# Products paired on row halves in the first mixer, and a class-ordered copy written by ScalarE in the dilated mixer

## The chip, the cores and the metric

The kernel runs as one program on one core of a Trainium2 chip. Five engines matter: TensorE (PE: matrix products; PEld is its weight loads), VectorE (DVE), ScalarE (ACT), GpSimd (POOL) and SyncE (SP), which issues the DMAs. Each works through its own queue in order and waits on semaphores for the others. The metric is the device time of one execution in microseconds; the median of three runs of the kernel before is 3385.5 us (3381.23 to 3389.09).

## What is computed

Two transformer blocks run one after the other on 512 tokens of width 1024. The first has two layers: a mixer and a convolutional FFN each. Its first layer's mixer joins a chunked gated linear attention and a differential attention; its second layer's mixer is a dilated attention. The second block (FFNs, a grouped-query attention with pooling, a gated MLP mixer) is not touched by the change. What the change touches, cut short:

```python
# gated linear attention, chunks of 64 tokens, 4 heads, dk = 64, dv = 128
att = jnp.where(causal, jnp.einsum('bhnik,bhnjk->bhnij', q_d, k_d), 0.0)
o_intra = jnp.einsum('bhnij,bhnjv->bhniv', att, vc)
o = o_intra + jnp.einsum('bhnik,bhnkv->bhniv', q_d, states)      # state product

# differential attention, 4 heads of two parts c, dh = 64, blocks of 128 queries
s = jnp.einsum('bhcqd,bhckd->bhcqk', qblk, kt)                   # score products
p = jax.nn.softmax(jnp.where(kpos[None, :] <= qpos[:, None], s, -jnp.inf), axis=-1)
w = p[:, :, 0] - lam * p[:, :, 1]

# dilated attention: three patterns (128, 1), (512, 4), (2048, 16); dilation 4 and 16 read
# keys, queries and values by residue class of the token (to_class)
```

## The kernel before

Activations stand with features on the 128 partitions and tokens along the row. Each weight product is done three times at reduced precision: operands are split into a high and a low part (`hh`, `hl`, `whi`, `wlo`, `mh`, `ml`), and high by high, low by high and high by low are summed (`mm3`, tiles `gm` and `gt`). ScalarE writes the high part of a weight tile (`whi`), VectorE the rest (`wlo`), from `raw` buffers that SyncE's DMAs fill; a new `raw` is loaded once the `wlo` that read the old one is done. Small products inside the mixers are plain float32; in the trace each of them is two matmul records, called two passes below.

The order of every engine's instructions is settled when the program is built. Mixers are written as tasks (Python generators), and a planner keeps a clock for each engine with a cost for each operation (class `Clock`). After every group of weight products (`tick`) it lets those tasks take a step whose inputs should be ready by TensorE's planned time, if enough of the eight PSUM banks are free. A task that ends earlier or later in the planned time, or takes its banks in another order, so moves the rows of all engines near it.

In the first mixer (`even_mixer`) `diff_unit` does one block of 128 queries of one head of the differential attention: for each of the two parts j it forms scores of `w` = 128, 256, 384 or 512 keys (tile `ds`, contraction over 64 of the 128 rows: rows 0 to 63 for j = 0, 64 to 127 for j = 1), adds the causal mask by a product with the identity (`mc`), then the softmax: a maximum (`mx`) and its scaled negative (`nb`) on VectorE, the exponential (`dp`) on ScalarE. VectorE then joins the two parts (`drc`, `dr2`, `dp`), TensorE transposes (`dt`), ScalarE evacuates, TensorE multiplies by the values (`po`). There are 4 heads by 4 blocks, 16 units. `gla_out` forms the output of one head of the gated linear attention, in four token tiles: a product over 128 rows (`oa<-att,av`), then one or two state products over 64 rows (`oa<-qd,state`), an evacuation (`oraw`); `o_norm` follows it (`osq`, `ss`, `hv`, `rb`).

In the dilated mixer (`odd_mixer`) the first pattern's keys, queries and values come first. After the queries the class-ordered copy of h (`hp`, tiles `ph` and `pl`, 16 tiles of 128x512) is written, which the second and third pattern read. VectorE then has four key norms (`k_norm`: `hv`, `ksq`, `rb`, `ok`) and four query scales (`q_scale`: `qv`, `cc`, `rs_t`, twelve small operations each) to do before the first softmax of the scores `os` (`nbs`, `pr`).

Of the kernel before, what the change touches and what calls it, by code (L numbers as in the profile page):

```python
# [14 lines left out]
AF = mybir.ActivationFunctionType  # L15
# [4 lines left out]
P = 128  # L20
# [4 lines left out]
NK = D // P  # L25
# [156 lines left out]
class Kern:  # L182
# [706 lines left out]
    def even_mixer(self):  # L889
        nc = self.nc  # L890
        h = self.hx
        H = [(h, S)]
        w = lambda i: ("ev_w_in", i)
        toks = [slice(t * P, (t + 1) * P) for t in range(4)]
        lam = self.cp.tile([P, 1], F32, name="lamv")
        kn, qs = {}, {}
        kh, qh = [], []
        pre = self.firsts([w(8), w(9), w(6)])
        for b in range(2):
            for m, ps in enumerate(pre[b]):  # L900
                kr = self.evac(ps, "bk")
                kh.append(self.spawn(self.k_norm(kr, kn, 2 * b + m, self.v("dk_gain"), self.c("bones"), 64, S)))
        for b in range(2):
            for m, ps in enumerate(pre[2] if b == 0 else [p[0] for p in self.gemm(w(7), NK, H)]):
                qh.append(self.q_scale(ps, qs, 2 * b + m, self.v("dq_gain"), self.c("bones2"), 2, 64))
        self.spawn(self.lam(lam))
        bv = [self.g("bv") for _ in range(4)]
        for b in range(2):
            for t, p in enumerate(self.gemm_tok(w(10 + b), NK, h, toks)):
                nc.scalar.activation(bv[t][:, b * 256:(b + 1) * 256], p, AF.Copy)  # L910
        ob, oa = {}, {}
        dn = []
        for hd in range(4):
            o = self.g("dor")
            us = [self.spawn(self.diff_unit(hd, n, qs, kn, bv, lam, o), (qh[hd], kh[hd])) for n in range(4)]
            dn.append(self.spawn(self.o_norm(o, ob, hd, self.v("diff_gain"), 1.0 - (0.8 - 0.6 * math.exp(0.0))), us))

        ps = self.gemm(("ev_w_ar",), NK, H, widths=(16,))[0][0]
        ar = self.g("ar")
        nc.vector.memset(ar[0:17], 1.0)  # L920
        nc.scalar.activation(ar[0:16], ps[0:16], AF.Copy)
        gs = {}
        la = self.spawn(self.log_decay(ar, gs))
        gs["q"] = [self.evac(p[0], "qd", scale=0.125) for p in self.gemm(w(0), NK, H)]
        gs["k"] = [self.evac(p[0], "kr") for p in self.gemm(w(1), NK, H)]
        gs["av"] = av = [self.g("av") for _ in range(4)]
        for b in range(2):
            for t, p in enumerate(self.gemm_tok(w(2 + b), NK, h, toks)):
                nc.scalar.activation(av[t][:, b * 256:(b + 1) * 256], p, AF.Copy)
        gl = self.spawn(self.gla(gs), [la])  # L930
        sg = []
        for b in range(2):
            for m, ps in enumerate(self.gemm(w(4 + b), NK, H)):
                t = self.g("sg")
                nc.scalar.activation(t, ps[0], AF.Silu)
                sg.append(t)
        self.tables(LNEXP)
        gn = [self.spawn(self.gla_out(gs, hd, sg[hd], oa), [gl]) for hd in range(4)]
        self.finish(dn)
        self.proj_out("ev_w_out", None, [ob[i] for i in range(4)], first=4)  # L940
        self.finish(gn)
        self.final(("ev_w_out",), [oa[i] for i in range(4)], None)
# [91 lines left out]
    def diff_unit(self, hd, n, qs, kn, v, lam, o):  # L1034
        nc = self.nc
        q, cc = qs[hd]
        k = kn[hd]
        w = (n + 1) * P
        pr, sm = [], self.s("dsm", 2)
        for j in range(2):  # L1040
            s = self.ps("ds", w)
            r = slice(j * 64, j * 64 + 64)
            self.mm(s, q[r, n * P:(n + 1) * P], k[r, :w], stop=False)
            self.mm(s[:, n * P:], self.mbf["ident"], self.mbf["mc"], start=False)
            p = self.g("dp")
            nb = self.s("nb", 1)
            self.softmax(s, cc[:, 2 * n + j:2 * n + j + 1], p[:, :w], sm[:, j:j + 1], nb)
            pr.append(p)
        yield
        rc = self.s("drc", 2)  # L1050
        nc.vector.reciprocal(rc, sm)
        r2 = self.s("dr2", 1)
        nc.vector.tensor_mul(r2, rc[:, 1:2], lam)
        nc.vector.tensor_scalar(pr[1][:, :w], pr[1][:, :w], r2, None, op0=OP.mult)
        nc.vector.scalar_tensor_tensor(pr[0][:, :w], pr[0][:, :w], rc[:, 0:1], pr[1][:, :w],
                                       op0=OP.mult, op1=OP.subtract)
        yield
        pt = self.ps("dt")
        for j in range(n + 1):
            nc.tensor.transpose(pt[:, j * P:(j + 1) * P], pr[0][:, j * P:(j + 1) * P], self.ident)  # L1060
        wt = pr[1]
        nc.scalar.activation(wt[:, :w], pt[:, :w], AF.Copy)
        yield
        po = self.ps("po", P)
        for j in range(n + 1):
            self.mm(po, v[j][:, hd * P:(hd + 1) * P], wt[:, j * P:(j + 1) * P], start=(j == 0), stop=(j == n))
        nc.scalar.activation(o[:, n * P:(n + 1) * P], po, AF.Copy)
        yield
# [101 lines left out]
                    st[c, n + 1] = prev = s  # L1170
                yield

    def gla_out(self, gs, hd, sg, oa):
        nc = self.nc
        av, att, st, qd = gs["av"], gs["att"], gs["st"], gs["q"]
        c, r = hd // 2, slice((hd % 2) * 64, (hd % 2) * 64 + 64)
        o = self.g("oraw")
        for t in range(4):
            p = self.ps("oa", P)
            self.mm(p, av[t][:, hd * P:(hd + 1) * P], att[t][:, hd * P:(hd + 1) * P], stop=False)  # L1180
            ns = [n for n in (2 * t, 2 * t + 1) if n]
            for n in ns:
                self.mm(p[:, (n % 2) * 64:(n % 2) * 64 + 64], st[c, n][r, :], qd[c][r, n * 64:n * 64 + 64],
                        start=False, stop=(n == ns[-1]))
            nc.scalar.activation(o[:, t * P:(t + 1) * P], p, AF.Copy)
            yield
        yield from self.o_norm(o, oa, hd, self.v("gla_gain"), gate=sg)


    def odd_mixer(self):  # L1190
        nc, a = self.nc, self.a
        h = self.hx
        w = lambda i: ("od_w_in", i)

        def cls(x):
            return x.rearrange("p (r m) -> p r m", r=4)

        def clsps(x):
            return x.rearrange("p (m r) -> p r m", r=4)
# [4 lines left out]
        prob, kt, qs = {}, {}, {}  # L1204
        su, val = [], {}
        hp = []

        def values(gi, b, hh):
            if b == 0:
                val[gi] = [self.g("ov") for _ in range(4)]  # L1210
            sls = [slice(t * P, (t + 1) * P) for t in range(4)]
            for t, p in enumerate(self.gemm_tok(w(gi * 6 + 4 + b), NK, hh, sls)):
                nc.scalar.activation(val[gi][t][:, b * 256:(b + 1) * 256], p, AF.Copy)

        for gi in range(3):
            kh = []
            if gi == 0:
                pk = self.firsts([w(2), w(3), w(0)])
            H = [(hp if gi else h, S)]
            for b in range(2):  # L1220
                for m, ps in enumerate(pk[b] if gi == 0 else [p[0] for p in self.gemm(w(gi * 6 + 2 + b), NK, H)]):
                    k = self.g("ok")
                    nc.scalar.activation(k, ps, AF.Copy)
                    kh.append(self.spawn(self.k_norm(k, kt, (gi, 2 * b + m), self.v("od_k_gain"), self.ones, 128, S)))
            for b in range(2):
                for m, ps in enumerate(pk[2] if gi == b == 0 else [p[0] for p in self.gemm(w(gi * 6 + b), NK, H)]):
                    hd = 2 * b + m
                    qh = self.q_scale(ps, qs, (gi, hd), self.v("od_q_gain"), self.ones[:, 0:1], 1, 128)
                    prob[gi, hd] = [self.g("pr0"), self.g("pr1")] if gi == 0 else [self.g("pr")]
                    su.append(self.spawn(self.odd_scores(gi, hd, kt, qs, prob[gi, hd], sms, nbs), (kh[hd], qh)))  # L1230
            if gi == 0:

                for xs in h:
                    hp.append((self.h("ph"), self.h("pl")))
                    for x, y in zip(xs, hp[-1]):
                        nc.gpsimd.tensor_copy(cls(y), clsps(x))
                for b in range(2):
                    values(0, b, h)

        values(1, 0, hp)  # L1240
        self.finish(su)
        gs = {}
# [611 lines left out]
```

## Time and profile before

| what | value |
|---|---|
| median of three runs | 3385.5 us |
| the profiled execution, its own time | 3386.47 us |
| its span in the trace | 3384.7 us |
| mean granted TensorE clock | 0.993 of full speed |
| PE busy | 3327.9 us (98%) |
| PEld busy | 2898.5 us (86%) |
| DVE busy | 2113.2 us (62%) |
| ACT busy | 1251.6 us (37%) |
| POOL busy | 28.0 us (1%) |
| differential attention, from the first to the last score product | about 107 to 185 us |
| outputs of the gated linear attention | 244 to 280 us |
| class-ordered copies on POOL | 724.8 to about 747 us |

Busy time is the time in which an engine has an instruction under way; TensorE's matmuls overlap in their pipeline, so for its speed one compares the starts of consecutive rows. The granted clock has two levels in the trace, 1.2 and 2.4 GHz, shown as 0.5 and 1.0. All records carry the line of one helper (L172), so groups are told apart by the tiles' names: `ds<-bk,q` writes `ds` from `bk` and `q`.

### The profile page before, as it was taken

The numbers are of one execution on the slowest core, as the hardware profiler recorded it, in microseconds if no ns is written. First come the engines' busy times: TensorE is split into PE (matmuls) and PEld (weight loads), VectorE is DVE, ScalarE is ACT, GpSimd is POOL, SyncE is SP. The second block draws the span as 40 slices with busy tenths as digits, with TensorE's granted clock in tenths as the row PEclk, the third lists the DMA queues.
The fourth block names the chain that finished last, engine by engine and source line by source line (L and its number), as shares of the span: only waits on it lengthen the run. The fifth ranks groups of instructions, "written<-read, shape, count | busy, mean of one in ns | idle before, by whom it ended". The sixth has DMA issues, their size and how long they took to land.

```text
span 3384.7 us, 48370 instructions
## 1 busy us (share of the span) xinstructions
PE 3327.9 (98%) x19172; PEld 2898.5 (86%) x19172; DVE 2113.2 (62%) x4570; ACT 1251.6 (37%) x2526; POOL 28.0 (1%) x29
## 2 busy tenths in 40 slices
PE   7999999989999999999999989999999999999999
PEld 7688888888898888988888987988898889998888
DVE  5757988775669778764455867855663335463333
ACT  5554434334454334322112356422333223443231
POOL 0000000020000000000000000000000000000000
PEclk9999999999999999999999999999999999999999
DMA  3122444412224444443333311344532233222332
GB/s 112 63 63 80 128 141 131 131 63 74 70 88 125 132 136 131 129 146 111 125 119 119 94 42 44 122 153 144 163 100 85 95 100 100 94 89 93 100 99 70
DMA packets 105845, 355.73 MB, mean 105 GB/s; under 512 B 12673, under 2 KB 18962, under 8 KB 105618
## 3 DMA queue, kind: packets, MB, share of 16 engines
q1 hardware_dynamic: 105618, 352.64, 33.2%
q8 instruction: 150, 2.46, 0.3%
q14 instruction: 77, 0.63, 0.1%
HBM read 350.50 MB, written 2.10 MB: 104 GB/s over the span
## 4 chain that ended last, share of the span: by engine, by line
PE 89%; DVE 6%; ACT 3%; issue 1%; DMA 1%; SPq 0%; DVEq 0%; ACTq 0%
PE gm L172 81%; PE gt L172 4%; ACT ap L172 1%; PE ds L172 1%; DVE wlo L172 1%; PE ss L172 1%; DVE nt L172 1%; PE oa L172 1%; DVE amx L172 0%; DVE rs_t L172 0%; PE os L172 0%; ACT L172 0%; DVE ksq L172 0%; DVE x L172 0%; PE opo L172 0%
## 5 line engine op out<-in xcount | busy, mean ns | idle before, releaser
L172 PE MATMUL gm<-hh,whi 128*128 128x512 f32 (+1 forms) x2872 | 1041.0, 362 | 4.9 <-ACT hh L172 4.1
L172 PE MATMUL gm<-hl,whi 128*128 128x512 f32 (+1 forms) x2872 | 1034.5, 360 | 1.2 <-DVE hl L172 1.2
L172 PE MATMUL gm<-hh,wlo 128*128 128x512 f32 (+1 forms) x2872 | 1031.9, 359 | 3.5 <-DVE wlo L172 3.4
L172 DVE TENSOR_TENSOR wlo<-raw,whi 128x512 fp32r<-128x512 f32 (+1 forms) x1028 | 661.7, 681 | 91.9 <-ACT whi L172 91.5
L172 ACT ACTIVATE whi<-raw 128x512 fp32r<-128x512 f32 (+1 forms) x1028 | 581.4, 617 | 291.6 <-PE gm L172 104.8
L172 PEld LDWEIGHTS gm<-hh,wlo 128*128 128x128 f32 x2872 | 543.9, 189 | 87.1 <-DVE wlo L172 4.2
L172 PEld LDWEIGHTS gm<-hh,whi 128*128 128x128 f32 x2872 | 544.7, 190 | 73.5 <-ACT hh L172 4.4
L172 PEld LDWEIGHTS gm<-hl,whi 128*128 128x128 f32 x2872 | 544.7, 190 | 68.4 <-DVE hl L172 1.8
L172 PE MATMUL gm<-mh,whi 128*128 128x512 f32 (+1 forms) x1696 | 577.5, 341 | 0.0
L172 PE MATMUL gm<-ml,whi 128*128 128x512 f32 (+1 forms) x1696 | 573.5, 338 | 1.2 <-DVE ml L172 1.2
L172 PE MATMUL gm<-mh,wlo 128*128 128x512 f32 (+1 forms) x1696 | 572.1, 337 | 0.0
L172 DVE TENSOR_TENSOR ga<-ga,gm 128x512 f32<-128x512 f32 (+1 forms) x110 | 68.1, 633 | 497.5 <-PE gm L172 328.4
L172 PEld LDWEIGHTS gm<-mh,wlo 128*128 128x128 f32 x1696 | 322.2, 190 | 34.8
L172 PEld LDWEIGHTS gm<-ml,whi 128*128 128x128 f32 x1696 | 322.5, 190 | 29.4 <-DVE ml L172 1.6
L172 PEld LDWEIGHTS gm<-mh,whi 128*128 128x128 f32 x1696 | 322.4, 190 | 29.1 <-issue 0.9
L172 ACT ACTIVATE ga<-gm 128x512 f32<-128x512 f32 (+1 forms) x110 | 58.8, 554 | 715.9 <-PE gm L172 715.9
L172 DVE SCALAR_TENSOR_TENSOR macc<-rawm,sc,macc 128x256 f32<-128x256 f32 x504 | 244.0, 484 | 15.4
L172 DVE SCALAR_TENSOR_TENSOR x<-gm,modt,x 128x256 f32<-128x256 f32 (+1 forms) x184 | 106.0, 608 | 226.3 <-PE gm L172 226.2
L172 PEld LDWEIGHTS gm<-hc,whi 128*128 128x128 f32 x736 | 136.0, 190 | 29.0 <-ACT whi L172 1.6
L172 DVE SCALAR_TENSOR_TENSOR cy<-gm,vec,cy 128x511 f32<-128x511 f32 (+1 forms) x176 | 127.8, 747 | 47.9 <-ACT cy L172 44.7
L172 PE MATMUL gm<-hc,whi 128*128 128x256 f32 x736 | 146.2, 282 | 1.4 <-ACT whi L172 1.4
L172 ACT ACTIVATE nsq<-x 128x256 f32<-128x256 f32 x160 | 60.8, 416 | 179.4 <-DVE x L172 175.9
(300 smaller groups left out, 3530.7 us busy)
## 6 DMA issues: line engine op xcount, KB each, us to landing
raw<-in_ffn_w_dram SPq DMA_DIRECT2D x256, 512.0 KB, 4.3
rawm<-in_w_mod_dram SPq DMA_DIRECT2D x144, 512.0 KB, 4.4
raw<-in_ffn_w_up_dram SPq DMA_DIRECT2D x88, 512.0 KB, 3.7
raw<-in_ffn_w_down_dram SPq DMA_DIRECT2D x40, 512.0 KB, 3.7
raw<-in_od_w_in_dram SPq DMA_DIRECT2D x36, 512.0 KB, 3.8
raw<-in_ev_w_in_dram SPq DMA_DIRECT2D x24, 512.0 KB, 3.9
raw<-in_w_in_c_dram SPq DMA_DIRECT2D x16, 512.0 KB, 4.1
raw<-in_w_in_a_dram SPq DMA_DIRECT2D x10, 512.0 KB, 4.5
```

The lines of the kernel that those rows point to most:

```text
L172: return f(*args, **kwargs)
```

## The change

In `diff_unit` both parts' score products are written first, on rows 0 to 63 and 64 to 127 and into two PSUM banks, then both mask products, then both softmaxes. `gla_out` takes two heads at a time: their two products over 128 rows, then their state products alternating between the row halves, then two evacuations; the norm of each head becomes a task of its own. In the dilated mixer the 16 copies move from POOL to ScalarE as a task at the front of the list, whose steps are 0.9 us of planned time apart, and the end of the first pattern's values waits (in the plan) for that task.

```diff
--- before.py
+++ after.py
@@ -935,7 +935,12 @@
                 nc.scalar.activation(t, ps[0], AF.Silu)
                 sg.append(t)
         self.tables(LNEXP)
-        gn = [self.spawn(self.gla_out(gs, hd, sg[hd], oa), [gl]) for hd in range(4)]
+        gn = []
+        for c in range(2):
+            os = [self.g("oraw") for _ in range(2)]
+            go = self.spawn(self.gla_out(gs, c, os), [gl])
+            gn += [self.spawn(self.o_norm(o, oa, 2 * c + j, self.v("gla_gain"), gate=sg[2 * c + j]), [go])
+                   for j, o in enumerate(os)]
         self.finish(dn)
         self.proj_out("ev_w_out", None, [ob[i] for i in range(4)], first=4)
         self.finish(gn)
@@ -1037,11 +1042,14 @@
         k = kn[hd]
         w = (n + 1) * P
         pr, sm = [], self.s("dsm", 2)
-        for j in range(2):
-            s = self.ps("ds", w)
+
+        ss = [self.ps("ds", w) for _ in range(2)]
+        for j, s in enumerate(ss):
             r = slice(j * 64, j * 64 + 64)
             self.mm(s, q[r, n * P:(n + 1) * P], k[r, :w], stop=False)
+        for s in ss:
             self.mm(s[:, n * P:], self.mbf["ident"], self.mbf["mc"], start=False)
+        for j, s in enumerate(ss):
             p = self.g("dp")
             nb = self.s("nb", 1)
             self.softmax(s, cc[:, 2 * n + j:2 * n + j + 1], p[:, :w], sm[:, j:j + 1], nb)
@@ -1170,21 +1178,24 @@
                     st[c, n + 1] = prev = s
                 yield
 
-    def gla_out(self, gs, hd, sg, oa):
+    def gla_out(self, gs, c, os):
+
         nc = self.nc
         av, att, st, qd = gs["av"], gs["att"], gs["st"], gs["q"]
-        c, r = hd // 2, slice((hd % 2) * 64, (hd % 2) * 64 + 64)
-        o = self.g("oraw")
         for t in range(4):
-            p = self.ps("oa", P)
-            self.mm(p, av[t][:, hd * P:(hd + 1) * P], att[t][:, hd * P:(hd + 1) * P], stop=False)
+            ps = [self.ps("oa", P) for _ in range(2)]
+            for j, p in enumerate(ps):
+                hd = 2 * c + j
+                self.mm(p, av[t][:, hd * P:(hd + 1) * P], att[t][:, hd * P:(hd + 1) * P], stop=False)
             ns = [n for n in (2 * t, 2 * t + 1) if n]
             for n in ns:
-                self.mm(p[:, (n % 2) * 64:(n % 2) * 64 + 64], st[c, n][r, :], qd[c][r, n * 64:n * 64 + 64],
-                        start=False, stop=(n == ns[-1]))
-            nc.scalar.activation(o[:, t * P:(t + 1) * P], p, AF.Copy)
+                for j, p in enumerate(ps):
+                    r = slice(j * 64, j * 64 + 64)
+                    self.mm(p[:, (n % 2) * 64:(n % 2) * 64 + 64], st[c, n][r, :], qd[c][r, n * 64:n * 64 + 64],
+                            start=False, stop=(n == ns[-1]))
+            for o, p in zip(os, ps):
+                nc.scalar.activation(o[:, t * P:(t + 1) * P], p, AF.Copy)
             yield
-        yield from self.o_norm(o, oa, hd, self.v("gla_gain"), gate=sg)
 
 
     def odd_mixer(self):
@@ -1204,6 +1215,12 @@
         prob, kt, qs = {}, {}, {}
         su, val = [], {}
         hp = []
+
+        def turn():
+            for xs, ys in zip(h, hp):
+                for x, y in zip(xs, ys):
+                    yield self.time() + 0.9
+                    nc.scalar.activation(cls(y), clsps(x), AF.Copy)
 
         def values(gi, b, hh):
             if b == 0:
@@ -1230,12 +1247,11 @@
                     su.append(self.spawn(self.odd_scores(gi, hd, kt, qs, prob[gi, hd], sms, nbs), (kh[hd], qh)))
             if gi == 0:
 
-                for xs in h:
-                    hp.append((self.h("ph"), self.h("pl")))
-                    for x, y in zip(xs, hp[-1]):
-                        nc.gpsimd.tensor_copy(cls(y), clsps(x))
+                hp += [(self.h("ph"), self.h("pl")) for _ in range(NK)]
+                turned = self.spawn(turn(), front=True, banks=0)
                 for b in range(2):
                     values(0, b, h)
+                self.finish([turned])
 
         values(1, 0, hp)
         self.finish(su)
```

The first place is TensorE's queue at the first unit of head 0 of the differential attention. Before:

```order
L172 MATMUL gm_1161<-hh_129,wlo_1030 16x512
L172 MATMUL ds_1169<-bk_671,q_681 128x128
L172 LDWEIGHTS bf_ident_216
L172 MATMUL ds_1169<-bf_mc_218,bf_ident_216 128x128
L172 MATMUL ds_1178<-bk_671,q_681 128x128
L172 LDWEIGHTS bf_ident_216
L172 MATMUL ds_1178<-bf_mc_218,bf_ident_216 128x128
```

Now (`ds_1169` is part 0, `ds_1170` part 1):

```order
L172 MATMUL gm_1161<-hh_129,wlo_1030 16x512
L172 MATMUL ds_1169<-bk_671,q_681 128x128
L172 MATMUL ds_1170<-bk_671,q_681 128x128
L172 LDWEIGHTS bf_ident_216
L172 MATMUL ds_1169<-bf_mc_218,bf_ident_216 128x128
L172 LDWEIGHTS bf_ident_216
L172 MATMUL ds_1170<-bf_mc_218,bf_ident_216 128x128
```

The score product of the second part has moved ahead of the first part's mask product, so that two products on different row halves stand next to each other. All 16 units read like this.

The second place is TensorE's queue in the outputs of the gated linear attention. The rows of before are token tile 1 of head 0 (`oa_2556`) and of head 1 (`oa_2561`), then token tile 2 of the same heads (`oa_2566`, `oa_2571`). Before:

```order
L172 MATMUL oa_2556<-att_2378,av_1874 128x128
L172 MATMUL oa_2556<-qd_1641,state_2439 128x64 x2
L172 MATMUL oa_2561<-att_2378,av_1874 128x128
L172 MATMUL oa_2561<-qd_1641,state_2439 128x64 x2
L172 MATMUL oa_2566<-att_2408,av_1875 128x128
L172 MATMUL oa_2566<-qd_1641,state_2439 128x64
L172 MATMUL oa_2566<-qd_1641,state_2440 128x64
L172 MATMUL oa_2571<-att_2408,av_1875 128x128
```

Now token tile 2 of heads 0 and 1 (`oa_2602`, `oa_2603`), then of heads 2 and 3 (`oa_2612`, `oa_2613`):

```order
L172 MATMUL oa_2602<-att_2433,av_1834 128x128
L172 MATMUL oa_2603<-att_2433,av_1834 128x128
L172 MATMUL oa_2602<-qd_1625,state_2464 128x64
L172 MATMUL oa_2603<-qd_1625,state_2464 128x64
L172 MATMUL oa_2602<-qd_1625,state_2465 128x64
L172 MATMUL oa_2603<-qd_1625,state_2465 128x64
L172 MATMUL oa_2612<-att_2433,av_1834 128x128
L172 MATMUL oa_2613<-att_2433,av_1834 128x128
```

The two products over 128 rows now follow each other, and the state products of the two heads, which stand on different row halves, alternate.

The third place is ScalarE's queue after the last query evacuation of the first pattern in the dilated mixer. Before:

```order
L172 ACTIVATE qsq_7279<-gm_7132 128x512
L172 ACTIVATE q_7281<-gm_7132,vec_93 128x512
L172 ACTIVATE pr0_7123,sms_6658<-os_7413,nbs_6659,cc_7228 128x128
L172 ACTIVATE pr0_7129,sms_6658<-os_7444,nbs_6659,cc_7260 128x128
L172 ACTIVATE whi_7463<-raw_7007 128x512
L172 ACTIVATE pr0_7123,sms_6658<-os_7479,nbs_6659,cc_7228 128x256
L172 ACTIVATE pr0_7129,sms_6658<-os_7487,nbs_6659,cc_7260 128x256
L172 ACTIVATE ov_7317<-gt_7321 128x256
```

Now:

```order
L172 ACTIVATE q_7281<-gm_7132,vec_93 128x512
L172 ACTIVATE ph_7285<-hh_6386 128x512
L172 ACTIVATE pl_7286<-hl_6387 128x512
L172 ACTIVATE ph_7287<-hh_6388 128x512
L172 ACTIVATE pr0_7123,sms_6658<-os_7380,nbs_6659,cc_7228 128x128
L172 ACTIVATE pl_7288<-hl_6389 128x512
L172 ACTIVATE ph_7289<-hh_6390 128x512
L172 ACTIVATE pr0_7129,sms_6658<-os_7413,nbs_6659,cc_7260 128x128
L172 ACTIVATE whi_7432<-raw_7007 128x512
L172 ACTIVATE pl_7290<-hl_6391 128x512
L172 ACTIVATE pr0_7123,sms_6658<-os_7436,nbs_6659,cc_7228 128x256
L172 ACTIVATE ph_7291<-hh_6392 128x512
```

Three copies stand ahead of the first exponential (`pr0`) and the other thirteen between the later ones.

## Rows read from the trace of the kernel before

**Rows 1.** The page: engines, and one of its costliest groups

```profile
PE 3327.9 (98%) x19172; PEld 2898.5 (86%) x19172; DVE 2113.2 (62%) x4570; ACT 1251.6 (37%) x2526; POOL 28.0 (1%) x29
...
L172 ACT ACTIVATE whi<-raw 128x512 fp32r<-128x512 f32 (+1 forms) x1028 | 581.4, 617 | 291.6 <-PE gm L172 104.8
```

**Rows 2.** Stretches, in us: length, busy by engine, PEclk, DMA share, GB/s

```profile
107.00:185.00 78.00, 78.00 (x363) 49.31 (x362) 56.73 (x152) 52.73 (x127) 0.00 (x0) 0.96 0.16 48
112.00:119.00 7.00, 7.00 (x15) 2.12 (x15) 5.04 (x15) 3.91 (x10) 0.00 (x0) 0.51 0.04 4
249.00:262.00 13.00, 13.00 (x36) 9.17 (x35) 1.39 (x2) 3.59 (x10) 0.00 (x0) 0.50 0.06 22
744.00:757.00 13.00, 10.31 (x62) 9.78 (x62) 11.40 (x53) 0.43 (x2) 3.73 (x4) 0.75 0.00 0
757.00:768.00 11.00, 9.40 (x53) 8.53 (x54) 4.01 (x12) 5.71 (x19) 0.00 (x0) 0.69 0.04 5
```

**Rows 3.** Waits of PE, 660 to 960 us: total, times, longest

```profile
PE os L172 <- DVE qv L172: 5.0, 1, 5.0
PE gt L172 <- ACT pr L172: 3.5, 2, 2.1
```

**Rows 4.** PE in order of time, score and mask products: start, length

```profile
107.23 0.49 PE L172 MATMUL ds<-bk,q 64*128 64x128 f32 x2
107.64 0.23 PE L172 MATMUL ds<-bf_mc,bf_ident 128*128 128x128 bf16 x1
107.80 0.48 PE L172 MATMUL ds<-bk,q 64*128 64x128 f32 x2
...
137.90 1.12 PE L172 MATMUL ds<-bk,q 64*128 64x512 f32 x2
138.96 0.23 PE L172 MATMUL ds<-bf_mc,bf_ident 128*128 128x128 bf16 x1
139.12 1.12 PE L172 MATMUL ds<-bk,q 64*128 64x512 f32 x2
```

**Rows 5.** PE in order of time, products on row halves next to each other

```profile
226.98 1.71 PE L172 MATMUL attp<-qd,enb 64*128 64x128 f32 x16
228.62 0.50 PE L172 MATMUL gm<-hh,whi 128*128 128x512 f32 x1
...
239.98 0.65 PE L172 MATMUL kv<-av,el 64*64 64x128 f32 x12
```

**Rows 6.** PE in order of time, outputs of the gated linear attention

```profile
245.19 0.43 PE L172 MATMUL oa<-qd,state 64*128 64x64 f32 x2
245.56 0.49 PE L172 MATMUL oa<-att,av 128*128 128x128 f32 x2
245.97 0.66 PE L172 MATMUL oa<-qd,state 64*128 64x64 f32 x4
246.56 0.49 PE L172 MATMUL oa<-att,av 128*128 128x128 f32 x2
```

**Rows 7.** DVE, then PE, in order of time, first unit of head 0

```profile
113.50 0.35 DVE L172 SCALAR_TENSOR_TENSOR dp<-dp,drc 128x128 f32<-128x128 f32 x1
...
116.12 0.42 PE L172 MATMUL dt<-cst,dp 128*128 128x128 f32 x1
```

**Rows 8.** DVE in order of time, key norms and query scales

```profile
723.57 0.69 DVE L172 TENSOR_TENSOR ksq<-ksq,hv 128x512 f32<-128x512 f32 x1
...
741.71 1.46 DVE L172 SCALAR_TENSOR_TENSOR rb<-ksq,rb 128x512 f32<-128x512 f32 x1
...
749.24 0.15 DVE L172 TENSOR_SCALAR qv<-qst 128x4 f32<-128x4 f32 x1
...
751.50 0.15 DVE L172 TENSOR_SCALAR qv<-qst 128x4 f32<-128x4 f32 x1
```

**Rows 9.** ACT, then PE, in order of time, first exponential and the wait for it

```profile
756.57 0.46 ACT L172 ACTIVATE pr<-os,nbs,cc 128x128 f32<-128x128 f32 x1 [23.64 <-DVE nbs L172]
...
757.17 0.53 PE L172 MATMUL gt<-whi,hh 128*128 128x256 f32 x1 [2.06 <-ACT pr L172]
```

## The prediction

> **What bounds the kernel now.** I read the page first: TensorE is busy in 98% of the span, the others far less [rows 1]. So the time is TensorE's work, plus what the clock takes from it, plus the few places where it waits. Next I read the stretches that the change touches [rows 2]. From 107 to 185 us, the differential attention, TensorE is busy for 78.00 of 78 us and waits for nobody; VectorE is busy for 56.73 us, 73%. A product taken out here shortens the span by its whole length as long as the softmax keeps up. The outputs of the gated linear attention (249 to 262) read the same way, with VectorE nearly idle. The dilated mixer does not: from 744 to 757 TensorE is busy for only 10.31 of 13 us. The list of waits [rows 3] names it: 5.0 us for VectorE's `qv`, 3.5 us for ScalarE's `pr`. Last I read the granted clock in the same rows. It is at the lower level, 1.2 GHz, for 7 us from 112, for 13 us from 249, and for part of 744 to 768 (0.75 over 13 us, 0.69 over 11). A stretch at the lower level costs half its length, so the first mixer loses (7 + 13) / 2 = 10 us by the clock and the dilated one 13 x 0.25 + 11 x 0.31 = 6.7 us.
>
> **Score products in pairs.** At full clock one product of 128 keys takes 0.41 us from its start to the mask's, and the mask 0.16 us to the next start; with 512 keys it is 1.06 and 0.16 [rows 4]. In equal steps 256 and 384 keys take 0.63 and 0.84. A unit now pays twice product and mask: 2 x (0.57 + 0.79 + 1.00 + 1.22) = 7.16 us for a head's four units, 28.6 us for four heads. If the two products on different row halves run beside each other, a unit pays one product, one mask at 0.16 and a second mask behind it. That second mask has no row of its own; 128 columns of one bf16 pass are 0.05 us at 2.4 GHz, and its upper bound is the 0.16 of the first (1.8 us more over 16 units). I take 0.05, because nothing has to change over between two like products. That gives 0.62 + 0.84 + 1.05 + 1.27 = 3.78 us a head, 15.1 us in all: 13.5 us less.
>
> Do they run beside each other? Two kinds of product in this trace already stand on different parts of the array [rows 5]. Sixteen passes of `attp` over 64 rows take 1.64 us up to the next product. One after the other, with the same lead as the score product (0.41 us for the first two, then 0.22 for each further two, from the step between 128 and 512 keys), they would take 0.41 + 7 x 0.22 = 1.95 us. Twelve passes of `kv` on quarters take 0.58 us from 239.98 to the next start at 240.56 (the row's own 0.65 us has the drain in it), where 0.41 + 5 x 0.22 = 1.5 us would be serial. So halves and quarters do overlap, `kv` almost fully, `attp` in part because its second half begins late. In the new order the second product's two passes follow at once. The Trainium skill ("TensorE: Matmul & The Clock Gate", section "The mechanism") speaks against the full gain: matmuls start and end strictly in program order. By that rule the second pass of part 0 holds up the first of part 1, and a unit pays three passes instead of two; this is a rival below. The short time of `kv` does not look like it.
>
> **Linear attention outputs.** One token tile of a head pays 0.41 us for the product over 128 rows and 0.59 us for two state products (0.37 for the single one of the first tile) [rows 6]: (0.78 + 3 x 1.00) x 4 = 15.1 us. A pair will pay 0.41 + 0.22 for the two products over 128 rows and the states once: 0.63 + 0.37, then three times 0.63 + 0.59. That is 4.66 us for a pair and 9.3 us for both: 5.8 us less. The evacuations are the same number on ScalarE (3.59 of 13 us busy there [rows 2]). The norms as tasks of their own bring four small products together and cost TensorE nothing I can name; VectorE, busy 1.39 us of 13, hides them.
>
> **What VectorE then does.** The saved 13.5 us, and 3 us if the lower clock goes, leave about 61 us for the stretch that held 56.73 us of VectorE's work: 93%. It cannot be hidden whole. At the first unit VectorE's last operation ended at 113.50 + 0.35 = 113.85 and TensorE transposed at 116.12 [rows 7], a reserve of 2.3 us a unit. In head 0 each unit loses between 2 x 0.57 - 0.62 = 0.5 and 1.2 us on TensorE, 3.4 us over the head, so that reserve is used up by the first transposes: about 2.5 us of waiting in head 0 and about as much again, 3.5 us, over the three others, where weight products stand between. I put +6 us. The bounds are 0 (the plan's other products cover it) and +12 (nearly all of the saving). Queued behind a waiting transpose are weight products, which nobody else can give TensorE in the meantime.
>
> The Trainium skill ("TensorEngine Tiling (Array Packing)", section "PSUM Bottleneck") says that tiling speeds up TensorE but not the evacuation of PSUM, which may then be the bound. The 73% of VectorE agrees with that as a warning; by the rule alone, all of the gain above VectorE's reserve would be lost, which is the second rival.
>
> **The clock in the first mixer.** Which products bring the lower level is not shown by a row that isolates them. It falls while many short products over 64 rows stand among the others (112 to 119, 249 to 262). The change shortens both stretches but also adds waits. Bounds: all 10 us back, or none and more (third rival). Taking the middle: 5 us back.
>
> **Copies on ScalarE in the dilated mixer.** While POOL copies, VectorE's operations on 128x512 take 1.46 us instead of 0.69 us [rows 8]. There are four norms with four such operations, nearly all inside the copies, so without POOL they end about 14 x 0.75 = 10.5 us earlier. The query scales take 751.50 - 749.24 = 2.26 us each, and three instead of four now stand ahead of the first maximum. The first exponential, at 756.57 behind a ScalarE idle time of 23.64 us [rows 9], could come some 12 us earlier. The waits of 5.0 and 3.5 us [rows 3] then go, and the lower clock that goes with them (6.7 us): at most 15.2 us. What is late next is ScalarE. A copy of 128x512 there is not in the trace; the nearest row is `whi`, 617 ns [rows 1], so 16 copies are 10 us, inside those 23.64 us of idleness. The other end is POOL's own price: its 16 copies take some 22 us (724.8 to 747), 1.4 us each; at that, most of the idle time is used, and exponentials queue behind copies. Three copies stand ahead of the first exponential, 2 us; the other thirteen are between later ones, each holding them by 0.6 us, and `os` products wait for the banks that these free. So I take 11 us of the 15.2, from 6 to 14. SyncE's queue changes by two weight loads ahead of another; at 0.16 of the DMA engines' time [rows 2] I put 0 to 0.5 us, and take 0.
>
> **Sum.** -13.5 - 5.8 - 5 - 11 + 6 = -29.3 us, against the profiled execution's 3386.47: 3357.2 us. The median of the runs lies 1.0 us below that execution, so 3356 us.
>
> **Rivals.** First: passes go strictly in order, so only the middle two of four overlap. The score products then save a quarter of their time, 2 x 4 x (0.41 + 0.63 + 0.84 + 1.06) = 23.5 us / 4 = 5.9 us, the state products 2.5 us, VectorE has reserve (waits 1 instead of 6): 5.9 + 2.5 + 3 + 11 - 1 = 21 us, 3364 us. For it: `attp` took 1.64 of 1.95 us; against: `kv`.
>
> Second: the softmax becomes the bound and ScalarE's copies hold the exponentials. Waits of 12 us and 6 us gained in the dilated mixer: 13.5 + 5.8 + 5 + 6 - 12 = 18 us, 3367 us. For it: 93% leaves no room for a chain with four changes of engine a unit. Against: the plan has weight products between the units.
>
> Third, slower: the new waits and short products keep TensorE at 1.2 GHz through the whole differential attention. The gain without any clock term is 13.5 + 5.8 - 6 + 6 = 19 us; the lower level now takes 33 us of the two mixers. From 33 + 2 x 19 = 71 us on the change is a loss. All of 107 to 168 at the lower level and the rest as now adds (61 - 7) / 2 = 27 us: 8 us slower, 3393 us. For it: the level has already fallen once in this stretch, with TensorE waiting for nobody. Against: the many weight products between the units keep the other 71 us at full clock.
>
> Fourth: no overlap at all, and copies at 1.4 us that take back the rest: about 3385 us. Only `kv` and `attp` speak against it, plainly.
>
> **Chances.** Forecast 0.67, first rival 0.07, second 0.16, third 0.05, fourth 0.05. The forecast's own range, from the bounds of waits, clock and copies taken about half each, is 3346 to 3366 us. For 8 in 10 the range reaches up over the first two rivals to 3372 and down to all terms at their best (13.5 + 5.8 + 10 + 14 = 43 us) at 3343. About 0.2%, 7 us, is what can be told from no change. Forecast and the first two rivals are faster by more than that: 0.90; within: 0.05 (the fourth); slower: 0.05 (the third).
>
> **What would show it.** In the profile after: the two `ds` products of a unit start within a tenth of a microsecond of each other and the mask starts 0.41 to 1.06 us after the first; if instead 1.5 times that, the first rival holds. The `oa` pair takes 1.22 us a token tile. From 107 on the stretch is 65 to 70 us long with VectorE above 80%, and the list of waits has `dt` behind VectorE with 4 to 8 us; 12 us would be the second rival. The clock at 112 to 119 and around 245 is the least sure step. In the dilated mixer no VectorE operation on 128x512 takes over 1 us, ScalarE's copies take about 0.62 us, and the waits `os` behind `qv` are gone. A lower clock over more than 71 us of the two mixers would make the prediction wrong in its sign.

## The result and the profile after

The changed kernel takes 3355.5 us (median of four runs, 3354.89 to 3357.4) where the kernel before takes 3385.9 in the same company: a ratio of 0.9912, 95% interval 0.9895 to 0.9929, 30 us less. The forecast was 3356 us. Its profiled execution has a span of 3353.4 us, 31.3 us under that of before. The engines' line of the page:

```profile
PE 3298.8 (98%) x19172; PEld 2881.8 (86%) x19172; DVE 2099.4 (63%) x4570; ACT 1267.7 (38%) x2544; POOL 5.5 (0%) x13
```

Both traces have 19,172 matmuls, so the same number of rows can be compared. Adding up the steps from one TensorE row's start to the next, between the same row numbers of both traces, shows where the time went: the first mixer takes 17.7 us less, the dilated one 13.0 us less, and 0.6 us is left elsewhere, where the order is the same (1.4 us less ahead of the first mixer, some of it given back later).

TensorE's rows of a first and a last score unit of a head, in order of time (start, length), which answer to [rows 4]:

```profile
105.86 0.49 PE L172 MATMUL ds<-bk,q 64*128 64x128 f32 x4
106.29 0.29 PE L172 MATMUL ds<-bf_mc,bf_ident 128*128 128x128 bf16 x2
106.50 0.70 PE L172 MATMUL ds<-bk,q 64*128 64x256 f32 x4
...
108.42 1.13 PE L172 MATMUL ds<-bk,q 64*128 64x512 f32 x4
109.48 0.29 PE L172 MATMUL ds<-bf_mc,bf_ident 128*128 128x128 bf16 x2
109.57 0.42 PE L172 MATMUL gm<-hh,whi 128*16 128x512 f32 x1
```

Four passes (x4) of 128 keys now reach the mask in 0.43 us, where two took 0.41 before; with 512 keys 1.06 us, as two did. The whole unit takes 0.64 and 1.15 us. The four single records of the first unit start at 105.863, 105.869, 106.076 and 106.083 us, and the first two are the longer ones (0.37 against 0.27 us), as the first pass of a product was before: the first passes of both parts start 6 ns apart. The outputs of the gated linear attention, token tile 2 of the first pair, against [rows 6]:

```profile
238.08 0.71 PE L172 MATMUL oa<-att,av 128*128 128x128 f32 x4
238.72 0.66 PE L172 MATMUL oa<-qd,state 64*128 64x64 f32 x8
239.31 0.38 PE L172 MATMUL oa<-att,av 128*128 128x128 f32 x1
```

A pair's tile takes 1.23 us, where one head's took 1.00. Stretches of the profile after (columns as in [rows 2]): the place of the first lower clock, the outputs, and the two stretches of the dilated mixer some 32 us earlier than before:

```profile
112.00:119.00 7.00, 6.83 (x44) 4.21 (x41) 6.58 (x20) 4.14 (x12) 0.00 (x0) 1.00 0.22 75
235.00:248.00 13.00, 13.00 (x105) 10.85 (x104) 4.73 (x9) 6.62 (x23) 0.00 (x0) 1.00 0.29 83
712.00:725.00 13.00, 13.00 (x110) 12.89 (x109) 9.71 (x45) 7.53 (x11) 0.00 (x0) 1.00 0.00 1
725.00:736.00 11.00, 10.48 (x82) 9.46 (x80) 4.54 (x13) 11.00 (x26) 0.00 (x0) 1.00 0.01 1
```

All four are at 2.4 GHz. What grew are TensorE's waits in the first mixer, 100 to 300 us (total, times, longest), 8.6 us against 2.0 before:

```profile
PE ss L172 <- ACT osq L172: 2.1, 1, 2.1
PE gm L172 <- DVE ml L172: 1.6, 4, 0.8
PE gt L172 <- ACT dp L172: 1.4, 2, 1.2
PE po L172 <- ACT dp L172: 1.3, 3, 0.7
PE gm L172 <- DVE hl L172: 1.2, 1, 1.2
PE dt L172 <- DVE dp L172: 0.8, 1, 0.8
PE dt L172 <- DVE drc L172: 0.2, 1, 0.2
```

The one stretch at the lower level that is left in this mixer, 3.4 us from 202.5, begins as the longest of these waits, the one for `osq`, ends.

In the dilated mixer the waits of [rows 3] are gone but for 0.5 us. VectorE's key norms, ScalarE's first copy and the first maximum and exponential, against [rows 8, 9] (two views, VectorE first):

```profile
707.38 0.69 DVE L172 TENSOR_TENSOR ksq<-ksq,hv 128x512 f32<-128x512 f32 x1
...
721.95 0.28 DVE L172 TENSOR_REDUCE mx<-os 128x1 f32<-128x128 f32 x1
```

```profile
713.78 1.18 ACT L172 ACTIVATE ph<-hh 128x512 fp32r<-128x512 f32 x1
...
722.52 0.46 ACT L172 ACTIVATE pr<-os,nbs,cc 128x128 f32<-128x128 f32 x1 [5.47 <-DVE nbs L172]
```

No norm is slowed any more. The first exponential comes at 722.52, 19.0 us earlier by what lies ahead of this mixer and another 15.0 us earlier in its own stage. This first copy on ScalarE takes 1.18 us; all 16 lie between 1.11 and 1.20.

**The clock over all runs.** Each run lists its span and mean granted clock; (1 - clock) x span is what the lower level cost it, at most: where TensorE stood waiting at that level, it cost nothing. Means over the runs, in us; the rest is the mean without this cost:

| kernel | runs | mean | lost to the clock | rest |
|---|---|---|---|---|
| before | 19 | 3385.4 | 24.4 | 3361.0 |
| changed | 4 | 3355.8 | 11.7 | 3344.1 |
| scores in pairs alone | 10 | 3379.9 | 24.3 | 3355.5 |
| outputs in pairs alone | 8 | 3376.1 | 17.7 | 3358.4 |
| copies on ScalarE alone | 6 | 3372.6 | 20.2 | 3352.4 |
| same row half | 4 | 3367.8 | 14.3 | 3353.5 |

Of the 30 us, 17 are work and waits, and 13 are the clock. The listed clock has three digits, so one run's loss is known to within 1.7 us; single runs of one kernel differ in it by up to 14 us (the last row).

### The profile page after: what moved, and what is told of

It is laid out like the page before. It is cut to its first block, busy times and chain, and to the rows that moved or that the text cites. A ratio compares the mean times of both kernels' runs of the same rounds, so it can differ in the third digit from the quotient of the medians.

```text
span 3353.4 us, 48371 instructions
## 1 busy us (share of the span) xinstructions
PE 3298.8 (98%) x19172; PEld 2881.8 (86%) x19172; DVE 2099.4 (63%) x4570; ACT 1267.7 (38%) x2544; POOL 5.5 (0%) x13
## 4 chain that ended last, share of the span: by engine, by line
PE 89%; DVE 7%; ACT 3%; issue 1%; DMA 0%; SPq 0%; DVEq 0%; ACTq 0%
PE gm L172 81%; PE gt L172 4%; ACT ap L172 1%; DVE wlo L172 1%; DVE nt L172 1%; PE ss L172 1%; DVE amx L172 1%; DVE x L172 0%; ACT L172 0%; DVE hl L172 0%; PE os L172 0%; DVE rs_t L172 0%; PE opo L172 0%; DVE rb L172 0%; DVE nsq L172 0%
## 5 line engine op out<-in xcount | busy, mean ns | idle before, releaser
L172 PEld LDWEIGHTS gm<-mh,whi 128*128 128x128 f32 x1696 | 322.4, 190 | 29.3 <-issue 1.3
```

The costliest lines, as they stand in the source:

```text
L172: return f(*args, **kwargs)
```

## Experiments

**Each part alone.** The first three kernels are the kernel before with one part of the change each: the new `diff_unit`; the new `gla_out` with its call; the new `odd_mixer`.

```diff
+            self.mm(s, q[r, n * P:(n + 1) * P], k[r, :w], stop=False)   # first kernel: diff_unit as changed
...
+            go = self.spawn(self.gla_out(gs, c, os), [gl])              # second: gla_out and its call
...
+                turned = self.spawn(turn(), front=True, banks=0)        # third: odd_mixer
```

> The kernel before with the score products of the differential attention in pairs, nothing else. Theory (each unit pays one product instead of two because the row halves run beside each other, and with both halves in use the granted clock does not fall at 112 us): 13 us of products and 3.4 us of clock less, about 5 us of new waits, so some 11 us below before, 3374 us; the stretch 112 to 119 at 2.4 GHz, the one at 249 to 262 still at 1.2 GHz. Rival (the clock fell for a reason of its own, not for the half-used array): the same products saved but 112 to 119 still at the lower level, some 8 us below before, 3378 us. Rival (the softmax is the bound): 4 to 6 us below before, 3380 us, with over 10 us of waits behind VectorE and ScalarE.

Measured: 3379.5 us, ratio 0.9985 (0.9975 to 0.9994), 6 us less. The rows fall as forecast: the score and mask products' steps go from 29.2 us (2.0 of them clock) to 14.2. But the mixer's waits rise from 2.0 to 6.7 us, and the clock gives nothing back. Stretches and waits of this kernel:

```profile
112.00:119.00 7.00, 6.50 (x40) 3.95 (x40) 6.61 (x19) 3.86 (x11) 0.00 (x0) 1.00 0.27 75
239.00:253.00 14.00, 14.00 (x42) 10.59 (x42) 1.29 (x2) 4.01 (x11) 0.00 (x0) 0.51 0.12 43
```

```profile
PE ss L172 <- ACT osq L172: 2.1, 1, 2.1
PE gt L172 <- ACT dp L172: 1.4, 2, 1.2
PE po L172 <- ACT dp L172: 1.3, 3, 0.7
```

The lower level is gone from 112 us, yet this execution has one of 3.4 us from 95.8, behind a wait of 1.8 us that both kernels have, and over ten runs the loss is 24.3 us, as before. So the theory's size was wrong: a clock stretch that disappears from one trace isn't a gain until the mean over runs shows it. The number is that of the softmax rival, but not its mechanism: it wanted over 10 us of waits. Of the 13.1 us of products, this trace gives back 1.4 in longer steps of the products between them, 4.7 in the mixer's waits and 1.3 in the dilated mixer's, which leaves 5.7 us.

> The kernel before with the outputs of the gated linear attention in head pairs and their norms as tasks, nothing else. Theory: 4.9 us of products and 6.8 us of clock (249 to 262 at 2.4 GHz) less, up to 2 us given back where the four norms come together: 10 us below before, 3376 us. Rival (the clock is not tied to these products): 3 to 5 us below before, 3382 us, with the lower level still there for 13 us near 249.

Measured: 3376.3 us, ratio 0.9974 (0.9964 to 0.9984), 9 us less, as the theory said. The lower level near 249 is gone, the one at 112 still there:

```profile
112.00:119.00 7.00, 7.00 (x14) 2.11 (x15) 5.06 (x16) 3.88 (x10) 0.00 (x0) 0.51 0.03 3
238.00:252.00 14.00, 14.00 (x119) 11.24 (x112) 4.28 (x11) 6.08 (x17) 0.00 (x0) 1.00 0.25 77
```

Here the runs agree with the trace: 17.7 us lost to the clock instead of 24.4, no run above 20.2. Of the 9 us, 6.7 are clock and 2.6 work: the rows gain the forecast 4.9 us, and two waits for `hl` behind the mixer (1.6 us) and longer ones in the dilated mixer (0.7 us) take part of it back. The kernel has the pairs and the norms as tasks; which of the two brings the clock back isn't separated.

> The kernel before with the class-ordered copies on ScalarE, spaced, nothing else. Theory (the parts are independent, since the planner meets the dilated mixer in the same state): all of the 13.0 us that this mixer gained with the whole change, 3373 us; no wait of os behind qv, no lower clock between 740 and 768. Rival (part of the gain came from the first mixer's changed plan): 6 to 9 us, 3378 us.

Measured: 3372.6 us, ratio 0.9966 (0.9953 to 0.9978), 13 us less; the dilated mixer's rows take 13.0 us less, what they took less with the whole change. The three parts add up: 5.9 + 9.1 + 12.8 = 27.8 us of 30, or 5.5 + 2.6 + 8.6 = 16.7 of 16.9 without the clock.

**Same order, no overlap.** The changed kernel with part 1 of each softmax and the second head of each pair reading the first row half. All engines' queues read as in the changed kernel.

```diff
-            r = slice(j * 64, j * 64 + 64)
+            r = slice(0, 64)
             self.mm(s, q[r, n * P:(n + 1) * P], k[r, :w], stop=False)
...
-                    r = slice(j * 64, j * 64 + 64)
+                    r = slice(0, 64)
                     self.mm(p[:, (n % 2) * 64:(n % 2) * 64 + 64], st[c, n][r, :], ...
```

> The changed kernel with the second score product of each unit, and the state products of the second head of each pair, reading rows 0 to 63 like the first (so part 1 of each softmax repeats part 0, and the second head takes the first one's state). Order, banks and instruction counts are those of the changed kernel, only the overlap of row halves is gone. Theory: the 13 and 4.9 us of products come back, the clock falls again at the score products and the outputs (5 to 10 us), and 5 us of the new waits go: 3355 + 18 + 7 - 5 = 3375 us. Rival (the new order, not the overlap, made the gain): within 3 us of the changed kernel, 3355 to 3358 us.

Measured: 3368.6 us (3361.68 to 3372.35), 13 us above the changed kernel, 9.4 without the clock: neither theory's number. TensorE's rows of a unit of 128 keys:

```profile
106.32 0.71 PE L172 MATMUL ds<-bk,q 64*128 64x128 f32 x4
106.96 0.28 PE L172 MATMUL ds<-bf_mc,bf_ident 128*128 128x128 bf16 x2
107.18 1.13 PE L172 MATMUL ds<-bk,q 64*128 64x256 f32 x4
```

The unit takes 0.86 us: more than the 0.64 with overlap, but less than the 2 x 0.57 of before. So the gain has two sources. The steps of the score and mask products add up to 27.2 us before (at full clock), 22.6 us here, 14.2 us with overlap: 4.6 us come from setting like products next to each other, 8.4 us from the overlap. For the outputs it is 14.1, 12.3 and 9.2 us: 1.8 and 3.1. A single unit shows what a changeover between kinds of product costs: two score products apart take 2 x 0.41 us, together 0.64; two masks apart 2 x 0.16, together 0.22. That is 0.28 us a unit, 4.5 us over the 16. The waits hardly went (6.9 us instead of 8.6), and in this one trace the clock stays up at the score products and the outputs (the lower level stands in this mixer for 3.4 us, from 210.2), so the half-used array alone doesn't bring the lower level there, and the lower level stayed away although nothing overlapped; over its four runs the loss was between 6.7 and 20.2 us, too wide to say more.

**Which part of the copies' move matters.** The runs from here on had the kernel before at 3383.5 us in their company (3385.8 for the last two kernels), so a difference of 2 us from the changed kernel's 3355.5 says little; the rows of the traces don't depend on it. Two kernels change only `odd_mixer` of the changed kernel: the copies back on POOL as the spaced task, and all on ScalarE at once.

```diff
-                    nc.scalar.activation(cls(y), clsps(x), AF.Copy)
+                    nc.gpsimd.tensor_copy(cls(y), clsps(x))
```

```diff
-                    yield self.time() + 0.9
                     nc.scalar.activation(cls(y), clsps(x), AF.Copy)
+            yield
...
                 turned = self.spawn(turn(), front=True, banks=0)
+                self.step(turned)
```

> The changed kernel with the class-ordered copies back on GpSimd, but still as the spaced task at the front of the list. Theory (the copies cost by slowing VectorE, which then is late for the first softmax): VectorE's operations on 128x512 take 1.4 us again while they run, the wait of os behind qv is back with 3 to 5 us, and 8 to 12 us of the 13 us of this mixer are lost: 3365 us. Rival (the gain came from where the copies stand and how they are spaced, not from the engine): within 3 us of the changed kernel, 3355 to 3358 us.

Measured: 3362.5 us (3361.35 to 3364.46), 7.0 us above the changed kernel; the dilated mixer's rows take 7.1 us more than there. That is the theory at a little under its size. The wait is back, with it 6.8 us at the lower clock from 728.8, and VectorE is slowed where POOL copies (groups of VectorE, 715 to 735 us: busy, mean ns; then TensorE's wait, 660 to 960):

```profile
L172 DVE SCALAR_TENSOR_TENSOR ok<-ok,vec,rb 128x512 f32<-128x512 f32 x2 | 3.2, 1586 | 0.1
```

```profile
PE os L172 <- DVE qv L172: 4.1, 3, 2.8
```

> The changed kernel with the 16 copies on ScalarE all at once where GpSimd's stood, not spaced. Theory (ScalarE was idle for 23.6 us there, and 16 copies of 0.62 us fit): the first exponential comes at most 2 us later, 0 to 3 us lost: 3357 us. Rival (the spacing carries the gain, because exponentials queue behind a block of 10 us): waits of TensorE for pr of 5 us or more, 3362 us or more.

Measured: 3359.7 us (3358.57 to 3361.13), 4.2 us above the changed kernel, between the two theories; the dilated mixer's rows take 4.1 us more. TensorE waits for exponentials behind the block (its wait, then ScalarE's last copy and first exponential):

```profile
PE os L172 <- ACT pr L172: 3.6, 2, 3.4
```

```profile
731.92 1.09 ACT L172 ACTIVATE pl<-hl 128x512 fp32r<-128x512 f32 x1
732.91 0.44 ACT L172 ACTIVATE pr<-os,nbs,cc 128x128 f32<-128x128 f32 x1
```

So of the 13 us, 7 are the engine, and without spacing 4 of the 13 would have been lost. The expectation of 16 x 0.62 us was too short: the block lasts 16.5 us, from 716.46, and the first exponential starts right at its end. In the changed kernel, whose first copy is 2.7 us earlier, it starts at 722.52.

**Trying for more.** One kernel sets the `attp` products alternately on the row halves; the next tells the planner of the overlap as well; two put the log-decay task to the front, on either of these.

```diff
-            for j in range(2):
-                p = self.ps("attp")
-                for t in range(2):
-                    for c in range(2):
+            ps = [self.ps("attp") for _ in range(2)]
+            for t in range(2):
+                for c in range(2):
+                    for j, p in enumerate(ps):
                         self.mm(p[:, t * 256 + c * P:t * 256 + (c + 1) * P], ...
```

```diff
+        if engine == "tensor":
+            half = self.half(ins[0])
+            if half == 1 and self.prev == 0:
+                each = 0.01
+            self.prev = half
```

```diff
-        la = self.spawn(self.log_decay(ar, gs))
+        la = self.spawn(self.log_decay(ar, gs), front=True)
```

> The changed kernel with the attp products of the gated linear attention alternating between the row halves, as the state products do. Theory (adjacent products on different halves overlap fully; a block of eight passes followed by a block on the other half only in part): a group of 16 passes takes 1.0 us instead of 1.64, two groups, 1.3 us less: 3354 us, below what the timing can tell; the rows tell. Rival (attp overlaps as far as it can already): 1.64 us again.

Measured: 3356.4 us (3355.35 to 3357.11), the same as the changed kernel. The rows tell: 16 passes in 222.97 - 221.88 = 1.09 us instead of 1.64, two such groups, 1.1 us.

```profile
221.88 1.16 PE L172 MATMUL attp<-qd,enb 64*128 64x128 f32 x16
222.97 0.50 PE L172 MATMUL gm<-hh,whi 128*128 128x512 f32 x1
```

> As the one before, and the planner's cost of a product on rows 64 to 127 that follows one on rows 0 to 63 is set to 0.01 us, so that the plan expects the overlap. Theory (part of the 8.6 us of TensorE's waits in the first mixer stands there because the plan takes TensorE to be later than it is): the waits fall by 3 to 5 us, 3350 us. Rival (the waits are the softmax chain's own length): the order moves, the waits stay within 2 us of 8.6, 3353 to 3358 us.

Measured: 3360.5 us (3360.09 to 3363.63), slower than the changed kernel. The softmax waits fell as the theory said (`dt`, `po` and `gt`, from 3.7 to 1.6 us), but the outputs came later in TensorE's queue (from 245.4 us, not 236.2), and 9.9 us of waits for their norms stand at the end of the mixer:

```profile
PE gm L183 <- DVE ml L183: 7.1, 2, 4.2
PE gm L183 <- ACT mh L183: 2.8, 1, 2.8
PE po L183 <- ACT dp L183: 1.4, 2, 0.7
```

The clock is at the lower level for 13.7 us, from 269.4, as the first of these waits ends (columns as in [rows 2]):

```profile
269.40:283.00 13.60, 7.50 (x31) 6.91 (x32) 11.72 (x19) 6.60 (x11) 0.00 (x0) 0.50 0.00 0
```

TensorE works for 7.5 us of it, so it costs 3.8 us. In the traces the first mixer's products take 3.0 us less than in the changed kernel, its waits 3.1 us more and the clock 5.1 us more: what makes this kernel slower is the clock. Over its four runs it lost at most 21.0 us to it, against 11.7.

> The changed kernel with alternating attp products, and the log-decay task of the gated linear attention at the front of the list, so that its chain (decay, exponentials, attp, kv, outputs, norms) starts before the last softmax units instead of behind them. Theory (the 8.6 us of waits in the first mixer are chain lengths that show because TensorE now arrives earlier; an earlier start hides the part at the end of the mixer): the 2.1 us wait of ss and the 2.7 us around 270 to 300 go, the waits for the softmax stay or grow by 1: 3352 us. Rival (VectorE and ScalarE have no time left among the softmaxes): waits behind dp and drc grow by 4 us or more, 3357 us or more.

Measured: 3366.0 us, in the rival's range, but not by its mechanism: the waits behind `dp` and `drc` are 3.0 us, no more than in the changed kernel. The decay now waits 2.2 us for a weight that SyncE's queue brings late, the norms at the end still cost 3.1 us, and the lower level stands twice for 6.8 us among the softmaxes; in the first mixer's rows the clock costs 6.7 us more than in the changed kernel, the waits 3.0 us more.

```profile
PE gm L172 <- DVE ml L172: 3.1, 1, 3.1
PE la L172 <- DMA wa<-in_ev_wa2b_dram: 2.2, 1, 2.2
PE ds L172 <- ACT dor L172: 1.6, 1, 1.6
```

> The kernel whose plan expects the overlap, with the log-decay task at the front of the list. There the softmax waits were nearly gone, and 9.9 us of waits stood at the end behind the gated linear attention's norms. Theory (that chain was simply started late): these fall to 3 us or less, 3350 us. Rival (TensorE has too little other work left behind the outputs, wherever the chain starts): 6 us or more of waits stay there, 3356 us or more.

Measured: 3362.4 us, the rival again: 8.7 us of waits for the norms (`ml`, `mh`) stay at the end. No version found beats the changed kernel beyond what the runs can tell. Whether the 8.6 us of waits can be had by another order stays open.

## Why the prediction was right

- **Score products: -13.5 us; measured -13.1** (27.2 to 14.2 us at full clock). The rule of strict order, the first rival, is out: first passes of both parts start 6 ns apart. That part of this gain is the saved changeover and not the overlap (4.6 of 13) wasn't seen, though it was in the working: the 0.41 us of a first product carried it.
- **Outputs: -5.8 us; measured -4.9.** The size of a pair's tile was right (1.22 against 1.23 us); the rows of before, at full clock, add up to 14.1 us instead of 15.1.
- **New waits: +6 us; measured +6.6.** The sum was right, its parts were not, so its size is luck. Transposes wait 1.0 us, not 4 to 8; 2.7 us are behind the exponential or the evacuation (`dp`), 1.7 more than before is the wait of `ss`, 1.6 us more stands at `ml` and `hl`, beyond the softmaxes, and a wait of 0.4 us for `dor` is gone. VectorE is busy for 54.37 of 69.27 us from the first to the last score product, 78%, not 93%: the transposes don't come to a full VectorE.
- **Clock of the first mixer: -5 us; in the profiled executions -8.5** (10.2 to 1.7 us). This is the term that was mis-sized. Over the runs it is the outputs' part that returns it (6.7 us), not the scores' (0).
- **Not in the sum: +2 us.** The terms above add to -19.9 us, the mixer gained 17.7. The rest is in longer steps: those of `dt` and `ss` are 0.5 us longer each in sum, those of `po` 0.4, and others spread over the weight products. That they stand beside other kinds of product than before may be the cause; no run shows it.
- **Dilated mixer: -11 us; measured -13.0.** Waits fell by 8.0 us and the lower clock's cost by 5.5, and the steps got 0.6 us longer. The forecast's 15.2 counted 1.3 us twice: it put the clock at half of all the time at the lower level, 6.7 us, and TensorE stood waiting for 2.6 us of that time. The price of a copy was wrong by a factor of two (0.62, measured 1.18 us): `whi` reads and writes in order, the copy reads every fourth element, and that nearest row was no guide (no run changes the order alone). The spacing covered most of the error: without it 4.1 us come back.
- **SyncE: 0; nothing seen** in the changed kernel: no wait of TensorE for a DMA stands in the first mixer, and `la` starts at 190.2 us, at 190.4 before.

The total, -29.3 forecast and -31.3 in the profile, is right partly because errors of the clock (-3.5), the dilated mixer (-2), the execution's own 0.6 us, the outputs (+0.9), the waits (+0.6) and the unforeseen 2 us offset each other.

The second rival (softmax bound) shows in the scores' part alone: 13.1 us of products became 5.5 us of gain, and not all of the difference is waits for the softmax. In the changed kernel such waits (`dt`, and `dp`'s) are 3.7 of the 6.6 us. The third did not come, nor the fourth.

## What to carry to other kernels

Here two products on different row halves cost the time of one when they were next to each other in the queue, and grouping like products saved the changeover even without overlap; look for a block of passes on one half followed by a block on the other (alternating them saved 1.1 us here). What such a gain is worth is settled by the chain that then is late (5.5 of 13 us here), so count the waits, not only the products, and the clock over several runs. Telling the planner the right cost of a single operation didn't make this kernel faster.

## What was not expected of the hardware

A copy of 128x512 on ScalarE with every fourth element read took 1.18 us, against 0.62 for one in order. A score product between products of another kind paid 0.18 us that it didn't pay behind a like one: two passes 0.41 us, four 0.64. Waits of 9.9 us close together stood with 13.7 us at the lower clock, which cost another 3.8 us. And the slowing in the dilated mixer went both ways: in the trace of before, POOL's copies took 1.54 to 1.61 us beside VectorE's 128x512 operations (but for the first, 1.16), and 1.10 and 1.12 us when these had ended:

```profile
742.58 1.54 POOL L172 CAST ph<-hh 128x512 fp32r<-128x512 f32 x1
...
745.56 1.10 POOL L172 CAST ph<-hh 128x512 fp32r<-128x512 f32 x1
```
